# Decoder trunk on one core: block sums planned earlier in a second tile, a weight sum formed from other regions, and the first w_o weights asked for inside the branch loop

## The chip, the core and the metric

The kernel runs on one core of a Trainium2 chip. The metric is device time in microseconds (us): the median over runs of the whole kernel, one launch each. Engines are named as in the profile: PE (matrix products), PEld (weight loads of PE), DVE, ACT and POOL (elementwise work), SP (it issues the transfers; its queue reads SPq in the trace).

## The reference

Two layers of a decoder trunk run over a sequence of 1024 with a model width of 1024. Each layer has a mixer and a gated feed-forward part.

```python
def rmsnorm(x, g):
    y = xf * lax.rsqrt(jnp.mean(xf * xf, axis=-1, keepdims=True) + RMS_EPS)
    return (y * g).astype(x.dtype)
...
D_MODEL = 1024; SEQ = 1024; DEPTH = 2; HEAD_DIM = 64; D_FF = 2816
DSW_GROUPS = ((128, 1), (512, 4), (2048, 16))     # (window, dilation), 4 heads each
SB_HEADS = 4                                      # stick-breaking heads
...
# mixer, per layer:
#   h = rmsnorm(x, norm1) ; one projection w_in gives q/k/v of both branches and two gates
#   branch A: softmax attention in dilated windows with ALiBi, three groups mixed by their denominators
#   branch B: A[t,s] = sigmoid(z_ts) * prod_{s<j<t} (1 - sigmoid(z_tj)), o = A v
#   m = sigmoid(gate_a) * (o_a @ w_br[:OUT_A]) + sigmoid(gate_b) * (o_b @ w_br[OUT_A:])
#   x = x + m @ w_o
# feed-forward: up-projection, depthwise conv of the gate half, GELU, down-projection
```

All of it is in 32-bit floating point.

## The kernel before

**Precision.** Each fp32 operand is split into two parts of the type fp32r, `hi = copy(x)` on ACT (L129) and `lo = x - hi` on DVE (L130), by the helper `split`; a product of two operands is three matmuls (`hi*hi`, `lo*hi`, `hi*lo`). `piece(src)` splits a 128x512 region of weights into two new tiles.

**Tiles.** `H[n]` holds the normalised input h of token half n as `hh`, `hl`. Tiles come from pools by tag, and a new tile of a tag waits until the oldest buffer of that tag is no longer used. The tag "xa" has four buffers of 128x2048 (here: `h_sum`, and `on`, `ob_in`), "wr" two (`NRAW`; raw weights `w_raw`, `br_raw`, and the tile `u` of the pairs), "ql" two (`in_a`), "ot" is a tag with a single 128x1024 buffer (here: the zeros `none`, and `raw_c` at the start of a layer).

**The mixer.** Attention is cut into items: B00 to B17 (stick-breaking), N00 to N11 (near windows), T00 to T17 (far windows). `attend` goes through them and, between their steps, advances a `Dense` object, which yields the projections one matmul group at a time. PE's order is written out by hand in this way; the rows of PE are kept in the order of the program, while the other engines' instructions outside the feed-forward part are placed by a list scheduler. At each advance `aside()` takes one entry off the list `side`, if the item that the entry names is done.

**The pairs.** 28 pairs of projections (keys and queries, values, gates) go by a seven-product scheme on 2x2 blocks. One of the seven products is computed early by `ahead` and kept in DRAM. `pair_rest` computes the other six from the four 128x512 regions a11, a12, a21, a22 of the tile `in_a`: it forms weight sums on POOL and DVE, splits them (w6, w5, w7, then w3, w4), and multiplies them by sums of h. A pair's third weight sum, for w7, is made by POOL on L998, in the half `u2` of the tile `u`; the other half `u1` receives the kept product from DRAM. L1000 is `a21 += a22` (POOL), L1003 `a11 = a21 - a11` (DVE), L1006 `a11 = a12 - a11` (POOL). L855 is four copies (`fx`) that a far item puts on POOL.

**The sums of h.** `block_sums` fills `dense.side`: for each of the sums S[3], S[1], S[2], S[4] four items of 128x512. An item of S[3] and S[1] is three POOL operations (L906 to L908, function `first`) into one quarter of the tile `h_sum`, an item of S[2] and S[4] two DVE operations on that tile (L917, L918, `further`). `in_two` then splits the quarter into the tiles t_hi and t_lo. In `series(after, t, f, lag, gap)` item i starts at entry i*gap and is split at entry i*gap+lag, once the item named by `after` is done.

**The branches.** After the far items come the products with `w_br` (`br_raw`, four loads by `branch_in`, L1214), the gates read back from DRAM (`gin`, L1206) and, in layer 0, `residual_in`. The loop goes over 16 outputs i. Then come the products with `w_o`, whose weights are loaded in pieces by L140 in `wo_chunk`; the first step of the generator `wo[0]` asks for the first two of them and splits them.

Of the kernel before, what the change touches and what calls it, by code (L numbers as in the profile page):

```python
# [6 lines left out]
F32 = mybir.dt.float32  # L7
# [4 lines left out]
ALU = mybir.AluOpType  # L12
# [3 lines left out]
P = 128  # L16
T = 1024
D = 1024
KD = D // P
HF = 512  # L20
# [11 lines left out]
NRAW = 2  # L32
# [20 lines left out]
def trunk_kernel(ctx, tc, x, norm1, w_in, b_gate, w_br, w_o, norm2, w_up, conv_w, conv_b, w_down, norm_f, out, depth=None, probe=None):  # L53
    nc = tc.nc
    act, dve, pe, pool = nc.scalar, nc.vector, nc.tensor, nc.gpsimd
# [4 lines left out]
    sb = ctx.enter_context(tc.tile_pool(name="sb", bufs=1))  # L60
# [64 lines left out]
    def quarter(name, dtype=F32, c=HF):  # L125
        return sb.tile([P, 2048 // c, c], dtype, tag="xa", bufs=4, name=name)

    def split(hi, lo, src):
        act.copy(hi, src)  # L129
        dve.tensor_tensor(lo, src, f32(hi), ALU.subtract)  # L130
# [64 lines left out]
    class Dense:  # L195
# [29 lines left out]
        def at(self, ahead, f):  # L225
            self.later.setdefault(self.count + ahead, []).append(f)
# [203 lines left out]
    S, B = {}, {}  # L430
# [15 lines left out]
    def new_s(t):  # L446
        hi, lo = big("t_hi", F32R), big("t_lo", F32R)
        S[t] = [tuple(x.rearrange("p a (b c) -> p (a b) c", c=HF)[:, i, :] for x in (hi, lo)) for i in range(4)]
# [431 lines left out]
    def piece(src):  # L880
        hi = sb.tile([P, 512], F32R, tag="wh", bufs=4, name="w_hi")
        lo = sb.tile([P, 512], F32R, tag="wl", bufs=4, name="w_lo")
        split(hi, lo, src)
        return hi, lo
# [10 lines left out]
    def block_sums():  # L895


        keep = {}

        def first(t, a, b, i):  # L900
            if i == 0:
                if "r" not in keep:
                    keep["r"] = quarter("h_sum")
                new_s(t)
            r, (ah, al), (bh, bl) = keep["r"][:, i, :], a()[i], b()[i]
            pool.tensor_tensor(r, f32(al), f32(bl), ALU.subtract)  # L906
            pool.tensor_tensor(r, r, f32(ah), ALU.add)
            pool.tensor_tensor(r, r, f32(bh), ALU.subtract)  # L908

        def further(t, a, i):  # L910
            if t == 4:

                S[4] = half(0, 0)
            elif i == 0:
                new_s(t)
            r, (ah, al) = keep["r"][:, i, :], a()[i]
            dve.tensor_tensor(r, f32(ah), r, ALU.subtract)  # L917
            dve.tensor_tensor(r, r, f32(al), ALU.add)  # L918

        def in_two(t, i):  # L920
            split(*S[t][i], keep["r"][:, i, :])

        b11, b12, b21, b22 = (lambda n=n, k=k: half(n, k) for k in range(2) for n in (1, 0))
        todo = []

        def series(after, t, f, lag, gap):

            at = {}
            for i in range(4):
                at.setdefault(i * gap, []).append(lambda i=i: f(i))  # L930
                at.setdefault(i * gap + lag, []).append(lambda i=i: in_two(t, i))
            for k in range(3 * gap + lag + 1):
                todo.append((after, lambda fs=at.get(k, ()): [g() for g in fs]))

        series({"B17"}, 3, lambda i: first(3, b22, b12, i), 6, 5)
        series({"N01s"}, 1, lambda i: first(1, b12, b11, i), 6, 5)
        series({"N11s"}, 2, lambda i: further(2, b22, i), 1, 1)
        series({"plain", "01", "v0"}, 4, lambda i: further(4, b21, i), 1, 1)
        return todo

# [37 lines left out]
    def pair_rest(dense, l, offs, put, view, grid, kept):  # L978
        raw = []

        def load():
            raw.append(sb.tile([P, 4, 512], F32, tag="ql", bufs=2, name="in_a"))
            for c in range(2):
                nc.sync.dma_start(
                    raw[0][:, 2 * c : 2 * c + 2, :].rearrange("p a (k n) -> p (a k) n", n=P),
                    w_in[l][:, offs[c] : offs[c] + P].rearrange("(k p) n -> p k n", p=P),
                )

        def run():
            if not raw:  # L990
                assert dense.loads.pop(0) is load
                load()
            a11, a12, a21, a22 = (raw[0][:, i, :] for i in range(4))
            yield
            u = sb.tile([P, T], F32, tag="wr", bufs=NRAW, name="u")
            u1, u2 = u[:, HF:T], u[:, 0:HF]
            nc.sync.dma_start(u1, kept)
            pool.tensor_tensor(u2, a11, a21, ALU.subtract)  # L998
            yield
            pool.tensor_tensor(a21, a21, a22, ALU.add)  # L1000
            yield
            yield
            dve.tensor_tensor(a11, a21, a11, ALU.subtract)  # L1003
            w6 = piece(a11)
            yield
            pool.tensor_tensor(a11, a12, a11, ALU.subtract)  # L1006
            w5 = piece(a21)
            yield
            w7 = piece(u2)
            yield  # L1010
            u5 = small("u5")
            pa, pc = bank("ps", "i_a"), bank("ps", "i_c")
            yield from seven(pa, w6, S[2], True, True)
            r2 = u2
            dve.tensor_tensor(view(r2), view(u1), grid(pa), ALU.add)
            w3 = piece(a11)
            yield "turn"
            yield
            yield from seven(pc, w5, S[1], True, True)
            dve.tensor_tensor(view(u5), view(u1), grid(pc), ALU.add)  # L1020
            w4 = piece(a22)
            if dense.loads:
                dense.loads.pop(0)()
            dense.last(0)
            yield "turn"
            yield
            yield from seven(pa, w7, S[3], False, True)
            dve.tensor_tensor(view(u5), view(u5), grid(pa), ALU.add)
            put(1, 0, u5, False)
            yield "turn"  # L1030
            yield
            yield from seven(pc, w3, half(0, 1), False, True)
            dve.tensor_tensor(view(r2), view(r2), grid(pc), ALU.add)
            put(0, 0, r2, False)
            dense.last(1)
            yield "turn"
            yield
            for word in seven(pa, w4, S[4], False, True):
                yield "turn"
                yield  # L1040
            dve.tensor_tensor(view(u1), view(u1), grid(pa), ALU.add)
            put(1, 1, u1, False)
            yield

        return run, load
# [84 lines left out]
    def mixer(l, pending):  # L1130
# [58 lines left out]
        def in_two(nm):  # L1189
            for src in (R["ob" if nm == "b" else "on"],):  # L1190
                hi, lo = big("oh_" + nm, F32R), big("ol_" + nm, F32R)
                for n in range(2):
                    for c in range(2):
                        sl = slice(n * HF, (n + 1) * HF)
                        split(hi[:, c, sl], lo[:, c, sl], src[:, c, sl])
                oh[nm] = (hi, lo)

        branches()
        todo = [(n, e0 + i) for e0 in range(0, KD, 2) for n in range(2) for i in range(2)]
# [25 lines left out]
        wo = [wo_chunk(l, n, e) for n in range(2) for e in range(KD)]  # L1225
# [5 lines left out]
        if l == 0:  # L1231
            for n in range(2):
                new_x(n)
        next(wo[0])
        next(residual, None)

        order = [(i, ab) for ab in (1, 0) for i in range(AHEAD_B)]
# [2 lines left out]
        for i, ab in order:  # L1240
            n, e = todo[i]
            sl = slice(n * HF, (n + 1) * HF)
            if i not in seen:
                if e == 0:
                    new_h(n)
                if i % 4 == 0:
                    wb = wbs.pop(0)
                if l and i in X_AT:
                    x_in(X_AT.index(i) // 2, X_AT.index(i) % 2)
            gt = gts[i]  # L1250
            ec = slice((e % 2) * P, (e % 2 + 1) * P)
            if "ab"[ab] not in oh:
                in_two("a")
            o = bank("st"[ab], "br_ps")
            (wh, wl), (xh, xl) = wb[ab], oh["ab"[ab]]
            for _ in product(o, [((wh[:, c, ec], wl[:, c, ec]), (xh[:, c, sl], xl[:, c, sl])) for c in range(2)]):
                pass
            with tc.high_priority(offset=AHEAD):
                dve.tensor_tensor(gt[:, ab, :], gt[:, ab, :], o, ALU.mult)
            seen[i] = seen.get(i, 0) + 1  # L1260
            if seen[i] == 1:
                continue
            m = small("mrg")
            dve.tensor_tensor(m, gt[:, 0, :], gt[:, 1, :], ALU.add)
            late.append((n, e, m))
            if len(late) > 1:
                merged(*late.pop(0))
            gate_in(i + 3)
            if i % 4 == 1:
                branch_in(i + 3)  # L1270
            next(residual, None)
# [586 lines left out]
```

## Time and profile before

| | before |
|---|---|
| median of 3 runs | 2748.46 us (2747.33 to 2750.36) |
| profiled execution | 2750.43 us |
| its span | 2748.6 us |
| mean granted PE clock | 0.993 |
| PE busy | 2672.8 us, 97% |
| DVE busy | 2096.1 us, 76% |
| ACT busy | 1328.1 us, 48% |
| POOL busy | 694.2 us, 25% |

PE is busy nearly all of the span, so a change can shorten the kernel only by the time that PE waits, by PE running at a higher granted clock, or by less work for PE. The work on PE is the same in both kernels. Rows of the timeline read: start in us, duration in us, engine, line, operation, output <- input, size, count, and in brackets the idle time of that engine just before with what ended it.

### The profile page before, as it was taken

What the parts mean: (1) busy time and instruction counts of PE and PEld (TensorE: products, weight loads), DVE (VectorE), ACT (ScalarE), POOL (GpSimd) and SP (SyncE); (2) the same over time, 40 slices, a digit from 0 to 9 for tenths busy, and PEclk for the clock granted to TensorE, in tenths of its full rate; (3) what the DMA queues carried; (4) which work ended last, traced back from release to release, by engine and by line L of the source; (5) the groups of instructions that cost most, each with busy time, mean ns of one, the idle gap of its engine ahead of it and who ended that gap; (6) DMA issues with size and microseconds to landing.
All of it is one profiled execution on the core that took longest, in us unless ns stands there. A gap on an engine that the chain in (4) does not pass through costs nothing. (4 is left out here: it accounts for less than half of the span.)

```text
span 2748.6 us, 36975 instructions
## 1 busy us (share of the span) xinstructions
PE 2672.8 (97%) x13098; PEld 2232.0 (81%) x13098; DVE 2096.1 (76%) x3132; ACT 1328.1 (48%) x2458; POOL 694.2 (25%) x509
## 2 busy tenths in 40 slices
PE   8998999999999999999999989999899999999999
PEld 8877777888888888888888778878788888888888
DVE  5887866775689888897658877666758888988865
ACT  5665534455455545432345655334545455554225
POOL 1004122212224433321210051221222333443110
PEclk9999999999999999999999999999999999999999
DMA  4023379764334443688411234897632434446863
GB/s 152 26 85 108 121 215 238 197 206 148 88 123 149 150 155 139 218 325 318 157 35 47 81 100 136 238 233 196 226 103 79 143 139 164 156 143 245 332 250 123
DMA packets 397637, 445.72 MB, mean 162 GB/s; under 512 B 21660, under 2 KB 318988, under 8 KB 395916
## 3 DMA queue, kind: packets, MB, share of 16 engines
q1 hardware_dynamic: 397452, 443.35, 50.4%
q8 instruction: 104, 1.70, 0.3%
q14 instruction: 81, 0.66, 0.1%
HBM read 300.61 MB, written 142.67 MB: 161 GB/s over the span
## 5 line engine op out<-in xcount | busy, mean ns | idle before, releaser
L130 DVE TENSOR_TENSOR w_lo<-up_a,w_hi 128x512 fp32r<-128x512 f32 x240 | 236.8, 993 | 20.1 <-ACT w_hi L129 20.1
L129 ACT CAST w_hi<-up_a 128x512 fp32r<-128x512 f32 x240 | 149.4, 623 | 183.8 <-PE u_a L890 45.8
L1614 DVE TENSOR_TENSOR x<-x,d_ps 128x512 f32<-128x512 f32 (+1 forms) x228 | 152.2, 671 | 78.1 <-PE d_ps L1608 77.3
L1345 POOL TENSOR_TENSOR cv<-cv 128x512 f32<-128x512 f32 x88 | 131.8, 1508 | 248.6 <-DVE cv L1340 138.7
L130 DVE TENSOR_TENSOR w_lo<-w_raw,w_hi 128x512 fp32r<-128x512 f32 x176 | 126.0, 719 | 68.8 <-ACT w_hi L129 68.3
L129 ACT CAST w_hi<-w_raw 128x512 fp32r<-128x512 f32 x176 | 109.2, 621 | 135.4 <-PE o_ps L156 66.5
L130 DVE TENSOR_TENSOR g<-cv,g 128x512 fp32r<-128x512 f32 x154 | 152.3, 990 | 5.3 <-ACT g L129 2.8
L129 ACT CAST w_hi<-in_a 128x512 fp32r<-128x512 f32 x112 | 68.6, 619 | 130.6 <-PE i_a L890 58.2
L1606 PE MATMUL d_ps<-gd_in,w_hi 128*128 128x512 f32 (+1 forms) x340 | 130.1, 383 | 1.5 <-ACT w_hi L129 1.2
L1608 PE MATMUL d_ps<-gd_in,w_lo 128*128 128x512 f32 (+1 forms) x340 | 129.8, 382 | 0.0
L1607 PE MATMUL d_ps<-gd_in,w_hi 128*128 128x512 f32 (+1 forms) x340 | 129.8, 382 | 0.0
L889 PE MATMUL u_a<-hh,w_hi 128*128 128x512 f32 x320 | 124.6, 389 | 0.3 <-DVE u L1496 0.3
L890 PE MATMUL u_a<-hl,w_hi 128*128 128x512 f32 x320 | 124.5, 389 | 0.0
L891 PE MATMUL u_a<-hh,w_lo 128*128 128x512 f32 x320 | 124.5, 389 | 0.0
L889 PE MATMUL u_a<-t_hi,w_hi 128*128 128x512 f32 x320 | 124.5, 389 | 0.0
L890 PE MATMUL u_a<-t_lo,w_hi 128*128 128x512 f32 x320 | 124.5, 389 | 0.0
L891 PE MATMUL u_a<-t_hi,w_lo 128*128 128x512 f32 x320 | 124.5, 389 | 0.0
L998 POOL TENSOR_TENSOR u<-in_a 128x512 f32<-128x512 f32 x28 | 37.9, 1355 | 328.1 <-DMA gs<-u 102.4
L1606 PE MATMUL d_ps<-gd_in,wd 128*128 128x512 f32 (+1 forms) x292 | 113.9, 390 | 0.0
L129 ACT CAST g<-cv 128x512 fp32r<-128x512 f32 x154 | 94.9, 616 | 38.0 <-POOL cv L1345 29.6
L1608 PE MATMUL d_ps<-gd_in,wd 128*128 128x512 f32 (+1 forms) x292 | 112.8, 386 | 0.0
L1607 PE MATMUL d_ps<-gd_in,wd 128*128 128x512 f32 (+1 forms) x292 | 112.8, 386 | 0.0
(390 smaller groups left out, 8715.4 us busy)
## 6 DMA issues: line engine op xcount, KB each, us to landing
gd<-g SPq DMA_DIRECT2D x154, 512.0 KB, 3.6
gd_in<-gd SPq DMA_DIRECT2D x154, 512.0 KB, 6.4
up_a<-in_w_up_dram SPq DMA_DIRECT2D x80, 512.0 KB, 5.3
in_a<-in_w_in_dram SPq DMA_DIRECT2D x56, 512.0 KB, 5.8
w_raw<-in_w_in_dram SPq DMA_DIRECT2D x104, 256.0 KB, 3.0
t_kq<-tk SPq DMA_DIRECT2D x64, 384.0 KB, 6.9
wd_raw<-in_w_down_dram SPq DMA_DIRECT2D x22, 1024.0 KB, 13.3
gin<-gs SPq DMA_DIRECT2D x32, 512.0 KB, 4.4
```

The costliest lines, as they stand in the source:

```text
L129: act.copy(hi, src)
L130: dve.tensor_tensor(lo, src, f32(hi), ALU.subtract)
L889: pe.matmul(o, w[0][:, c], rh, start=(first and i == 0), stop=False, skip_group_check=True)
L890: pe.matmul(o, w[0][:, c], rl, start=False, stop=False, skip_group_check=True)
L891: pe.matmul(o, w[1][:, c], rh, start=False, stop=(last and i == 3), skip_group_check=True)
L998: pool.tensor_tensor(u2, a11, a21, ALU.subtract)
L1345: return lambda: pool.tensor_tensor(dst, a, b, ALU.subtract)
L1606: pe.matmul(o[:, sub], wh[:, c], gh[:, sub], start=(i == 0 and k in (0, 4, 5)), stop=False, skip_group_check=True)
L1607: pe.matmul(o[:, sub], wh[:, c], gl[:, sub], start=False, stop=False, skip_group_check=True)
L1608: pe.matmul(o[:, sub], wl[:, c], gh[:, sub], start=False, stop=(i == m - 1), skip_group_check=True)
L1614: dve.tensor_tensor(x, x, o[:, sub], ALU.add)
```

## The change

1. **Sums of h.** The items 0 and 1 of S[3] go into a new tile `h_sum2` of the tag "ot" and are planned after item B14; items 2 and 3 stay in `h_sum` after B17, and the splits of all four get an explicit plan. The sums of S[1] get a lag of 7 and a gap of 6 in place of 6 and 5. The tiles t_hi and t_lo are allocated by the first split.
2. **Pairs.** The POOL operation `u2 = a11 - a21` is gone. After w6 (`a11 = a21 + a22 - a11`) POOL does `a12 -= a11` and `a11 = a22 - a11`, which is the old a11 - a21 again, and w7 is split from a11, w3 from a12. The tile `u` and the load of its half `u1` are asked for two steps later than the first operation was.
3. **Branches.** The first step of `wo[0]` is taken at i = 11 in the loop, not ahead of the loop.

```diff
         keep = {}
+        S.clear()
+
+        def at(t, i):
+            if t == 3 and i < 2:
+                if "o" not in keep:
+                    keep["o"] = sb.tile([P, 2, HF], F32, tag="ot", name="h_sum2")
+                return keep["o"][:, i, :]
+            if "r" not in keep:
+                keep["r"] = quarter("h_sum")
+            return keep["r"][:, i, :]
 
         def first(t, a, b, i):
-            if i == 0:
-                if "r" not in keep:
-                    keep["r"] = quarter("h_sum")
-                new_s(t)
-            r, (ah, al), (bh, bl) = keep["r"][:, i, :], a()[i], b()[i]
+            r, (ah, al), (bh, bl) = at(t, i), a()[i], b()[i]
...
         def in_two(t, i):
-            split(*S[t][i], keep["r"][:, i, :])
+            if t not in S:
+                new_s(t)
+            split(*S[t][i], at(t, i))
...
-        series({"B17"}, 3, lambda i: first(3, b22, b12, i), 6, 5)
-        series({"N01s"}, 1, lambda i: first(1, b12, b11, i), 6, 5)
+        plan({"B14"}, {0: [third(0)], 6: [third(1)]})
+        plan({"B17"}, {0: [third(2)], 1: [cast(0)], 4: [cast(1)], 6: [third(3)], 9: [cast(2)], 14: [cast(3)]})
+        series({"N01s"}, 1, lambda i: first(1, b12, b11, i), 7, 6)
         series({"N11s"}, 2, lambda i: further(2, b22, i), 1, 1)
...
             a11, a12, a21, a22 = (raw[0][:, i, :] for i in range(4))
             yield
+            pool.tensor_tensor(a21, a21, a22, ALU.add)
+            yield
+            yield
+            dve.tensor_tensor(a11, a21, a11, ALU.subtract)
+            w6 = piece(a11)
+            yield
+            pool.tensor_tensor(a12, a12, a11, ALU.subtract)
+            pool.tensor_tensor(a11, a22, a11, ALU.subtract)
+            w5 = piece(a21)
+            yield
             u = sb.tile([P, T], F32, tag="wr", bufs=NRAW, name="u")
             u1, u2 = u[:, HF:T], u[:, 0:HF]
             nc.sync.dma_start(u1, kept)
-            pool.tensor_tensor(u2, a11, a21, ALU.subtract)
-            yield
-            pool.tensor_tensor(a21, a21, a22, ALU.add)
-            yield
-            yield
-            dve.tensor_tensor(a11, a21, a11, ALU.subtract)
-            w6 = piece(a11)
-            yield
-            pool.tensor_tensor(a11, a12, a11, ALU.subtract)
-            w5 = piece(a21)
-            yield
-            w7 = piece(u2)
+            yield
+            w7 = piece(a11)
             yield
...
-            w3 = piece(a11)
+            w3 = piece(a12)
...
-        next(wo[0])
         next(residual, None)
...
             late.append((n, e, m))
+            if i == 11:
+                next(wo[0])
             if len(late) > 1:
```

In the changed kernel the lines have other numbers: L906 to L908 are L912 to L914, L944 is L960, L1000 is L1011, L1006 is L1017, the new POOL operation is L1018, L1003 is L1014, L1102, L1206 and L1214 are L1118, L1222 and L1230.

The first place is POOL in layer 0, from the zeros `none` to the first sums of h. The `ql` memsets are four tiles of the items' queries; `hl_109`, `hh_108` are the parts of H[0] and `hl_363` is one of H[1]. POOL before:

```order
L944 MEMSET none 128x1024
L545 MEMSET ql 64x1024
L546 MEMSET ql 64x1024
L545 MEMSET ql 64x1024
L546 MEMSET ql 64x1024
L906 TENSOR_TENSOR h_sum<-hl_109 128x512 x2
L907 TENSOR_TENSOR h_sum<-h_sum,hh_108 128x512 x2
L908 TENSOR_TENSOR h_sum<-h_sum,hh_108 128x512 x2
L906 TENSOR_TENSOR h_sum<-hl_109 128x512 x2
L907 TENSOR_TENSOR h_sum<-h_sum,hh_108 128x512 x2
L908 TENSOR_TENSOR h_sum<-h_sum,hh_108 128x512 x2
```

The same place on POOL after the change:

```order
L960 MEMSET none 128x1024
L912 TENSOR_TENSOR h_sum_2248<-hl_109 128x512 x2
L913 TENSOR_TENSOR h_sum_2248<-h_sum_2248,hh_108 128x512 x2
L914 TENSOR_TENSOR h_sum_2248<-h_sum_2248,hh_108 128x512 x2
L545 MEMSET ql 64x1024
L546 MEMSET ql 64x1024
L545 MEMSET ql 64x1024
L546 MEMSET ql 64x1024
L912 TENSOR_TENSOR h_sum<-hl_109 128x512 x2
L913 TENSOR_TENSOR h_sum<-h_sum,hh_108 128x512 x2
L914 TENSOR_TENSOR h_sum<-h_sum,hh_108 128x512 x2
```

Six operations, those of two items of S[3], stand ahead of the four memsets now, right behind the zeros; behind the memsets are 18 sum operations in place of 24.

The second place is POOL among the pairs of layer 0, where the first far item's four `fx` copies stand. POOL before:

```order
L1000 TENSOR_TENSOR in_a<-in_a 128x512
L1006 TENSOR_TENSOR in_a<-in_a 128x512
L998 TENSOR_TENSOR u<-in_a 128x512
L1000 TENSOR_TENSOR in_a<-in_a 128x512
L1006 TENSOR_TENSOR in_a<-in_a 128x512
L855 COPY fx<-sf 128x8x64 x4
L998 TENSOR_TENSOR u<-in_a 128x512
```

The same place on POOL after the change:

```order
L1011 TENSOR_TENSOR in_a<-in_a 128x512
L1017 TENSOR_TENSOR in_a<-in_a 128x512
L1018 TENSOR_TENSOR in_a<-in_a 128x512
L1011 TENSOR_TENSOR in_a<-in_a 128x512
L1017 TENSOR_TENSOR in_a<-in_a 128x512
L855 COPY fx<-sf 128x8x64 x4
L1018 TENSOR_TENSOR in_a<-in_a 128x512
```

A pair's three operations are now L1011, L1017, L1018, all on `in_a`, and the four `fx` copies stand between the second and the third operation of a pair instead of between two pairs.

The third place is SP at the change from the pairs to the branches in layer 1: `gs` takes the gates to DRAM, `x` reads the residual back, `w_raw` is a first w_o load. SP before:

```order
L1102 DMA gs<-u 128x512
L140 DMA w_raw<-in_w_o_dram 128x4x128
L404 DMA x_18173<-xs_86 128x2048
L1102 DMA gs<-u 128x512
L140 DMA w_raw<-in_w_o_dram 128x4x128
L1214 DMA br_raw<-in_w_br_dram 128x4x256
L1206 DMA gin<-gs 128x1024 x3
L1214 DMA br_raw<-in_w_br_dram 128x4x256
L1206 DMA gin<-gs 128x1024
L1214 DMA br_raw<-in_w_br_dram 128x4x256
```

The same place on SP after the change:

```order
L1118 DMA gs<-u 128x512
L1230 DMA br_raw<-in_w_br_dram 128x4x256
L1118 DMA gs<-u 128x512
L404 DMA x_18163<-xs_86 128x2048
L1230 DMA br_raw<-in_w_br_dram 128x4x256 x2
L1222 DMA gin<-gs 128x1024 x4
L140 DMA w_raw<-in_w_o_dram 128x4x128
L1222 DMA gin<-gs 128x1024 x2
L140 DMA w_raw<-in_w_o_dram 128x4x128
```

The last three `br_raw` loads now stand ahead of the four `gin` loads, and both w_o loads behind them.

More of the change, by code (lines that the diff above doesn't have):

```diff
@@ L913, in further @@
                 S[4] = half(0, 0)
-            elif i == 0:
-                new_s(t)
             r, (ah, al) = keep["r"][:, i, :], a()[i]
@@ L920, in in_two, with plan, third, cast @@
         def in_two(t, i):
-            split(*S[t][i], keep["r"][:, i, :])
+            if t not in S:
+                new_s(t)
+            split(*S[t][i], at(t, i))
         b11, b12, b21, b22 = (lambda n=n, k=k: half(n, k) for k in range(2) for n in (1, 0))
         todo = []
+        def plan(after, steps):
+            for k in range(max(steps) + 1):
+                todo.append((after, lambda fs=steps.get(k, ()): [g() for g in fs]))
         def series(after, t, f, lag, gap):
-            at = {}
+            steps = {}
             for i in range(4):
[L930 to L933, printed above, removed]
-        series({"B17"}, 3, lambda i: first(3, b22, b12, i), 6, 5)
-        series({"N01s"}, 1, lambda i: first(1, b12, b11, i), 6, 5)
+                steps.setdefault(i * gap, []).append(lambda i=i: f(i))
+                steps.setdefault(i * gap + lag, []).append(lambda i=i: in_two(t, i))
+            plan(after, steps)
+        def third(i):
+            return lambda: first(3, b22, b12, i)
+        def cast(i):
+            return lambda: in_two(3, i)
+        plan({"B14"}, {0: [third(0)], 6: [third(1)]})
+        plan({"B17"}, {0: [third(2)], 1: [cast(0)], 4: [cast(1)], 6: [third(3)], 9: [cast(2)], 14: [cast(3)]})
+        series({"N01s"}, 1, lambda i: first(1, b12, b11, i), 7, 6)
         series({"N11s"}, 2, lambda i: further(2, b22, i), 1, 1)
@@ L994, in run @@
             yield
[L995 to L998, printed above, removed]
-            yield
             pool.tensor_tensor(a21, a21, a22, ALU.add)
@@ L1005, in run @@
             yield
-            pool.tensor_tensor(a11, a12, a11, ALU.subtract)
+            pool.tensor_tensor(a12, a12, a11, ALU.subtract)
+            pool.tensor_tensor(a11, a22, a11, ALU.subtract)
             w5 = piece(a21)
             yield
-            w7 = piece(u2)
+            u = sb.tile([P, T], F32, tag="wr", bufs=NRAW, name="u")
+            u1, u2 = u[:, HF:T], u[:, 0:HF]
+            nc.sync.dma_start(u1, kept)
+            yield
+            w7 = piece(a11)
             yield
```

## The prediction

> **What bounds the kernel now.** I read the page first, then the list of PE's waits, then the timelines of POOL, ACT and PE at the three places that the change touches.
>
> ```profile
> PE 2672.8 (97%) x13098; PEld 2232.0 (81%) x13098; DVE 2096.1 (76%) x3132; ACT 1328.1 (48%) x2458; POOL 694.2 (25%) x509
> ```
>
> PE bounds the kernel: of the span of 2748.6 us it is idle for about 76. Its own instructions stay as they are, in the same order, so the change can win only parts of those 76 us and of the time in which PE ran at a lower granted clock. The list of its waits (engine, line, what it waited for: us in total, times, longest) says which of them the change can reach.
>
> ```profile
> PE z L584 <- DVE st L797: 8.0, 11, 1.3
> PE o L713 <- ACT p0h L129: 6.4, 2, 3.2
> PE o L815 <- DVE p1l L130: 6.1, 7, 1.8
> ```
>
> L713 is in the near items; L584 and L815 are mostly in the far items beside the pairs. Each is an attention operand that came late, and the question is why ACT and DVE were late with it.
>
> **Part 1, the sums of h.** POOL's timeline in layer 0:
>
> ```profile
> 30.94 0.96 POOL L944 MEMSET none<- 128x1024 f32 x1 [1.42 <-issue]
> 242.43 2.54 POOL L906 TENSOR_TENSOR h_sum<-hl 128x512 f32<-128x512 f32 x2 [21.15 <-PE sb_o L649]
> 255.84 2.53 POOL L908 TENSOR_TENSOR h_sum<-h_sum,hh 128x512 f32<-128x512 f32 x2
> 274.15 1.30 POOL L908 TENSOR_TENSOR h_sum<-h_sum,hh 128x512 f32<-128x512 f32 x1
> ```
>
> POOL has nothing of the sums to do until 242.43, when the last stick-breaking item releases the buffer, and then does all 24 sum operations in one burst to 275.45. ACT takes its queue in order, and the splits of the sums stand among the splits of the near items' probabilities; ACT, then PE:
>
> ```profile
> 257.16 0.62 ACT L129 CAST t_hi<-h_sum 128x512 fp32r<-128x512 f32 x1 [5.78 <-POOL h_sum L908]
> 261.65 0.48 ACT L129 CAST p0h<-t 128x384 fp32r<-128x384 f32 x1
> 258.56 0.39 PE L157 MATMUL q_ps<-hh,w_lo 128*128 128x512 f32 x1
> 262.18 0.58 PE L713 MATMUL o<-p0h,v 128*128 128x256 f32 x1 [3.23 <-ACT p0h L129]
> 264.03 0.58 PE L713 MATMUL o<-p0l,v 128*128 128x256 f32 x1 [1.26 <-DVE p0l L130]
> 266.11 0.63 PE L156 MATMUL q_ps<-hl,w_hi 128*128 128x512 f32 x1
> 268.78 0.48 PE L155 MATMUL q_ps<-hh,w_hi 128*128 128x512 f32 x1
> 282.30 0.79 PE L155 MATMUL r_ps<-hh,w_hi 128*128 128x512 f32 x1 [1.10 <-ACT q1s L967]
> 285.52 0.54 PE L155 MATMUL r_ps<-hh,w_hi 128*128 128x512 f32 x1
> ```
>
> ACT stands 5.78 us for a sum at 257.16, so p0h is cast only at 261.65, and PE has nothing from 258.95 on. Behind the wait PE runs slowly:
>
> ```profile
> 260.00:270.00 10.00, 6.56 (x23) 5.38 (x24) 8.60 (x19) 5.64 (x15) 10.00 (x7) 0.66 0.63 202
> 280.00:290.00 10.00, 8.31 (x35) 6.78 (x36) 9.24 (x16) 4.34 (x8) 0.00 (x0) 0.83 0.34 108
> 1640.00:1650.00 10.00, 8.32 (x45) 6.64 (x44) 9.89 (x18) 5.79 (x12) 0.00 (x0) 1.00 0.35 106
> ```
>
> These windows list the busy times of PE, PEld, DVE, ACT and POOL, then the granted clock, the DMA share and GB/s. The granted clock is 0.66 and 0.83 in the two windows of layer 0, and a matmul takes 0.63 in place of 0.39. The loss of the first stop, from the rows: 258.56 to 262.18 is 3.62, less the 0.23 that such a matmul takes in a full stream (start to start, 0.39 being its latency), 3.39; 262.18 to 264.03 is 1.85, less about 0.12 for half the columns, 1.73; the 4.75 from 264.03 to 268.78 at 0.43 a matmul in place of 0.23 lose 4.75 x (1 - 0.23/0.43) = 2.2. Together 7.3. Layer 1 has the same stop:
>
> ```profile
> 1624.13 0.58 PE L713 MATMUL o<-p0h,v 128*128 128x256 f32 x1 [3.21 <-ACT p0h L129]
> 1625.98 0.58 PE L713 MATMUL o<-p0l,v 128*128 128x256 f32 x1 [1.27 <-DVE p0l L130]
> ```
>
> so 14.6 for both. A second stop stands about 282.30: the window 280 to 290 has 1.69 us of idle PE, and its 3.22 us of slow matmuls (to 285.52) lose 3.22 x 0.465 = 1.5 (0.465 is 1 - 0.23/0.43), so 3.2; in layer 1 the window 1640 to 1650 has 1.68 of idle PE and a clock of 1.00. Together 4.9. This stop is DVE's work (9.24 and 9.89 of 10 busy), which stays, but POOL's burst ends about 8 us earlier now and takes DVE's share of it along, so I take half: 2.4.
>
> After the change six operations (two items) are done behind the zeros, more than 100 us before, and their splits wait for nothing. The cast that stood 5.78 us belongs to an item whose sum is now the first pair in the burst, or done; so the stop goes. The burst is 18 operations of about 1.3, some 24 us, so it ends near 267. What is new: in layer 1 the early sums take the tile "ot" when the vectors' transposes have left it, at the head of the layer, beside stick-breaking work on DVE. There is a row for such company:
>
> ```profile
> L130 DVE TENSOR_TENSOR t_lo<-h_sum,t_hi x24: 676/686/1755, 249.4 to 1684.8; 128x512 fp32r<-128x512 f32 x24
> ```
>
> A subtraction of two SBUF operands takes 0.686 and up to 1.755 beside POOL. Six early operations can delay six such by up to 1.07 each, 6.4 in all, of which PE's queued work hides a part. I take 1.5, bounds 0 and 6.4. Part 1: 14.6 + 2.4 - 1.5 = 15.5, bounds 8 (one layer's stop comes back) and 14.6 + 4.9 = 19.5.
>
> The Trainium skill, "SBUF — State Buffer", Who interferes with whom, says that a GpSimd instruction reading SBUF and a DVE instruction with two SBUF inputs exclude each other for a whole instruction, and whoever issues first wins; the row's 1.755 against 0.686 is about one POOL operation more, so the trace agrees. By it alone all six would cost a full operation, 6.4 in place of 1.5, and the sum would be 4.9 later, 2724.4. The same skill, "TensorE: Matmul & The Clock Gate", Part 1, has the clock fall to half only after an idle window of about 3.4 us; the drop at 282.30 came behind 1.10 us of waiting, so the measurement decides. By the page the 1.5 us of slow matmuls would not be there to win, and the sum would be later by half of it, 0.75.
>
> **Part 2, the pairs.** POOL's wait for `u`, DVE's for POOL, ACT's for DVE (us in total, times, longest where given):
>
> ```profile
> DVE in_a L1003 <- POOL in_a L1000: 38.6, 22, 4.3
> POOL u L998 <- DMA gs<-u: 102.4, 10, 13.8
> 478.67 0.69 DVE L1003 TENSOR_TENSOR in_a<-in_a 128x512 f32<-128x512 f32 x1 [2.54 <-POOL in_a L1000]
> 479.76 0.33 PE L584 MATMUL z<-t_kq 128*128 128x128 f32 x1 [1.29 <-DVE st L797]
> ```
>
> L998 needs a free "wr" buffer and stands ahead of L1000 on POOL; L1003 waits for L1000, and DVE's queue behind L1003 for it. At 478.67 one sees the end: PE waits 1.29 for a result that stood behind L1003. In after L1011 is first and needs no buffer. PE's two waits of this kind sum to 8.0 + 6.1 = 14.1; some of the 18 do not follow such an L1003. I take 11.5, bounds 4 and 14.1.
>
> New: w7 now needs L1018, which needs L1017 and the split of w6. At 1.30 for each POOL operation and 0.62 + 0.69 for the split the sum is ready some 0.69 + 1.31 + 1.30 = 3.3 us behind the start of L1003, in the best case. In the two rows on the cast of w7 below that cast comes 1.90 and 8.98 behind L1003; I count the tight ones at nothing, since L1003 itself comes earlier by such as the 2.99 that it waited there (0 to 1.4 for each if it does not). In one pair per layer the `fx` copies come between:
>
> ```profile
> 388.19 0.69 DVE L1003 TENSOR_TENSOR in_a<-in_a 128x512 f32<-128x512 f32 x1 [2.99 <-POOL in_a L1000]
> 390.09 0.61 ACT L129 CAST w_hi<-u 128x512 fp32r<-128x512 f32 x1
> 482.48 1.30 POOL L1006 TENSOR_TENSOR in_a<-in_a 128x512 f32<-128x512 f32 x1 [3.85 <-DVE w_lo L130]
> 487.74 2.74 POOL L855 COPY fx<-sf 128x512 f32<-128x512 f32 x4 [3.96 <-DVE sf L849]
> 487.65 0.62 ACT L129 CAST w_hi<-u 128x512 fp32r<-128x512 f32 x1 [1.92 <-PE i_c L890]
> ```
>
> `fx` ends at 490.48, L1018 at about 491.8, so w7's cast is 4.2 later than 487.65 and the casts of the far item's probabilities behind it on ACT as well; queued matmuls hide a part, and I take 2 for PE, near the middle of 0 and 4.2, in each layer: -4. Part 2: 11.5 - 4 = 7.5, bounds 4 - 8.4 = -4 and 14.
>
> **Part 3, the branches.** Layer 1, ACT, SP and PE:
>
> ```profile
> 1956.82 0.62 ACT L129 CAST w_hi<-w_raw 128x512 fp32r<-128x512 f32 x1 [5.58 <-DMA w_raw<-in_w_o_dram]
> 1962.77 0.62 ACT L129 CAST w_hi<-w_raw 128x512 fp32r<-128x512 f32 x1 [5.33 <-DMA w_raw<-in_w_o_dram]
> 1966.37 1.13 ACT L129 CAST br_w<-br_raw 128x512 fp32r<-128x512 f32 x2
> 1961.91 0.38 SPq L1214 DMA_DIRECT2D br_raw<-in_w_br_dram  x1
> 1967.56 0.50 PE L155 MATMUL br_ps<-oh_a,br_w 128*128 128x512 f32 x1 [3.10 <-ACT br_w L129]
> 1970.57 0.79 PE L157 MATMUL br_ps<-oh_a,br_w 128*128 128x512 f32 x1 [2.28 <-DVE br_w L130]
> 1975.00 0.52 PE L155 MATMUL br_ps<-oh_a,br_w 128*128 128x512 f32 x1
> ```
>
> ACT waits twice over 5 us for w_o weights that nobody needs yet, `br_raw` gets its buffer only at 1961.91, and PE waits 3.10 and 2.28, then runs slowly for 4.43 us. The loss is about 3.27 + 2.45 + 4.43 x 0.465 = 7.8 (0.17 of issue in each of the two). In after `br_raw` takes the buffer that the first w_o load had, some 9 us earlier. But three of these loads stand ahead of the four `gin` on SP's queue, the last waits for the splits of an earlier one, and the gates read by `gin` could be late. I leave 1.8 for it: 6, bounds 2 and 7.8. The w_o weights are asked for at i = 11 and used only behind i = 15, past four outputs of twelve matmuls, 48 x 0.23 = 11 us, against the 5.58 that ACT waited for such weights: nothing there. In layer 0 no such wait stands, nothing.
>
> **The sum.** 15.5 + 7.5 + 6 = 29.0 off 2750.43: 2721.4 for an execution like the profiled one. That was 1.97 above the median of the runs, 2748.46, so I predict 2719.5. The bounds of the parts together give a gain of 6 to 41; all at one end is unlikely, so the forecast's own range is 2708 to 2730.
>
> **The rivals.** *Smaller gain.* The sums' wait only moves: ACT and DVE are close to full between 242 and 285 (DVE 8.60 and 9.24 of 10), part 1 gives 8; SP's queue with three `br_raw` ahead of `gin` gives the branch stop back, 2; the pairs gain 3.5. Sum 13.5: 2735. *Larger gain.* The second stop goes whole, `fx` costs nothing because PE has work queued: 19.5 + 11.5 + 7.8 = 38.8: 2709.5. *Slower.* In every pair the cast of w7 now stands in ACT's queue behind a POOL sum that needs w6's split and one more operation, and behind w7 stand the far items' casts. If POOL is late in most of 28 pairs and PE loses 2 us each, that is 56 against the 33 that the rest gains (29.0 and the 4 already counted here): 23 slower, 2771. It decides from 33 / 28 = 1.2 us a pair. For it: ACT waited 55.9 us in all on L1003's result, by this row,
>
> ```profile
>   ACT w_hi L129: 55.9, 13
> ```
>
> so ACT's queue does stand for pair weights; against it: POOL is busy for 25% of the span, and in the quoted pair the cast has 8.98 us. *No effect.* What PE gains here it waits for a few us later at the next item: 2747.
>
> **How the numbers follow.** Forecast 0.50, smaller gain 0.18, larger 0.10, slower 0.15, no effect 0.05, something else 0.02, faster or slower. A measurement of this kernel tells about 0.2%, 5.5 us, from no change. The first three are faster by more, 0.80 with some of the rest; no effect is same, 0.05; slower 0.15. The range for 8 in 10 takes in the first three cases and reaches a little below the larger one: 2706 to 2739.
>
> **What would show it.** In the trace of after: the cast t_hi near 257 waits for less than 1 us, no wait of 3 us for p0h in the near items of either layer, and clock 1.00 in 260 to 270. The L1014 of the pairs wait for POOL under 10 us in all, against 38.6. ACT waits under 4 us for POOL L1018 except at `fx`, once a layer. In the branches of layer 1 no ACT wait for w_raw, and PE's two waits under 2 us together. The forecast is wrong if casts of w7 wait for POOL in many pairs and the far items' products behind them, or if a stop of 3 us with its slow matmuls stands in the near items as before.

## The result and the profile after

| | before | after |
|---|---|---|
| median of 16 runs | 2748.47 us (2745.29 to 2753.52) | 2756.39 us (2750.31 to 2766.18) |
| profiled execution | 2750.43 us | 2750.49 us |
| span | 2748.6 us | 2748.7 us |
| mean granted PE clock | 0.993 | 0.994 |

The changed kernel is slower: ratio 1.0027, 95% interval 1.0017 to 1.0036, some 8 us. The prediction was 29 us faster. The two profiled executions are equally long, because that of after is one of its shortest (5.9 under its median) and that of before lies 2.0 above its median. So the two traces show where time moved, and the size is taken from the medians.

PE's order is the same in both kernels, so the start of every matmul can be set against the start of the same matmul in the other trace. How far after lies behind before at several places:

```
place (time in before)                    after lies behind by
 240   before the near items, layer 0         0.5
 300   behind them                           -6.7
 640   behind the pairs, layer 0             -0.3
1420   head of layer 1                       -0.3
1440   20 us later                           +3.9
1620   before the near items, layer 1        +3.8
1660   behind them                           -1.8
1960   behind the pairs, layer 1             +7.6
1980   in the branches, layer 1              -0.6
2740   end                                   +0.1
```

The near items and the branches won 7, 6 and 8 us, as meant. The head of layer 1 lost 4, and the pairs lost 6 and 9. The list of PE's waits says the same (engine, line, what for: us in total, times, longest):

```profile
PE o L815 <- DVE p1l L130: 23.8, 16, 4.4
PE z L584 <- DVE st L797: 5.0, 2, 2.8
PE o L713 <- DVE p0l L130: 3.7, 8, 0.6
PE o L713 <- ACT p0h L129: 1.2, 2, 0.6
```

The wait for p0h fell from 6.4 to 1.2, the two of br_ps for weights are gone, but the wait for p1l in the far items rose from 6.1 to 23.8. The windows of after answer to those of before (busy times of PE, PEld, DVE, ACT, POOL, then granted clock, DMA share, GB/s):

```profile
260.00:270.00 10.00, 9.41 (x50) 7.53 (x49) 7.16 (x17) 8.07 (x20) 9.55 (x8) 1.00 0.50 134
460.00:470.00 10.00, 6.81 (x22) 5.25 (x21) 4.93 (x7) 1.20 (x2) 2.56 (x2) 0.69 0.41 125
500.00:510.00 10.00, 5.60 (x28) 4.64 (x28) 4.58 (x9) 3.19 (x9) 2.68 (x3) 0.91 0.89 217
1960.00:1970.00 10.00, 9.93 (x44) 7.94 (x43) 7.01 (x12) 2.16 (x4) 0.96 (x1) 1.00 0.90 291
```

Between 260 and 270 PE is now busy for 9.41 at full clock (6.56 at 0.66 before), between 1960 and 1970 for 9.93 (5.08). The new stops stand among the pairs: 460 to 470 at a clock of 0.69, and 500 to 510. This is the first one, on POOL, DVE, ACT and PE of after:

```profile
460.06 1.29 POOL L1011 TENSOR_TENSOR in_a<-in_a 128x512 f32<-128x512 f32 x1 [7.03 <-DMA in_a<-in_w_in_dram]
461.39 0.69 DVE L1014 TENSOR_TENSOR in_a<-in_a 128x512 f32<-128x512 f32 x1 [4.49 <-POOL in_a L1011]
457.98 0.48 ACT L129 CAST p1h<-t 128x384 fp32r<-128x384 f32 x1 [0.32 <-PE t L807]
463.89 0.54 DVE L130 TENSOR_TENSOR p1l<-t,p1h 128x384 fp32r<-128x384 f32 x1
464.49 0.58 PE L815 MATMUL o<-p1l,t_v 128*128 128x256 f32 x1 [3.19 <-DVE p1l L130]
466.15 0.63 PE L891 MATMUL i_a<-t_hi,w_lo 128*128 128x512 f32 x1
```

Read from below: PE waits 3.19 for p1l and then runs at 0.63 a matmul; p1l stands on DVE behind the difference L1014, though its own input p1h is there from 458.46 on; L1014 stands 4.49 for the sum L1011; and L1011 waits for the transfer that brings the pair's weights. The waits of the difference and of the first sum in the whole run, and of the third sum:

```profile
DVE in_a L1014 <- POOL in_a L1011: 57.5, 21, 4.5
POOL in_a L1011 <- DMA in_a<-in_w_in_dram: 104.0, 24, 10.3
POOL in_a L1018 <- DVE w_lo L130: 294.4, 28, 35.8
```

Before, the sum L1000 did not wait for the transfer but came later, behind L998 and its buffer. Now it stands some 17 us earlier (460.06; the same pair's L1000 is at 477.4 before) and reaches the weights while they are under way. Why DVE stands there is seen in DVE's order, around the difference of that pair (the tenth). Before:

```
L130 TENSOR_TENSOR p1l<-t_4720,p1h 128x384
L1033 TENSOR_TENSOR u<-u,i_c 128x512
L130 TENSOR_TENSOR w_lo<-u,w_hi 128x512
L130 TENSOR_TENSOR p1l<-t_4745,p1h 128x384
L1041 TENSOR_TENSOR u<-u,i_a 128x512
L130 TENSOR_TENSOR w_lo<-in_a,w_hi 128x512
L600 TENSOR_TENSOR ot<-o_4709,fold 64x512
L1015 TENSOR_TENSOR u<-u,i_a 128x512
L130 TENSOR_TENSOR w_lo<-in_a,w_hi 128x512
L1003 TENSOR_TENSOR in_a<-in_a 128x512
```

After:

```
L130 TENSOR_TENSOR p1l<-t_4723,p1h 128x384
L1014 TENSOR_TENSOR in_a<-in_a 128x512
L1049 TENSOR_TENSOR u<-u,i_c 128x512
L130 TENSOR_TENSOR w_lo<-in_a,w_hi 128x512
L130 TENSOR_TENSOR p1l<-t_4749,p1h 128x384
```

The difference moved up past eight operations of the pair before it and of the far item, p1l among them. The list scheduler put it where its sum seemed ready; the ring of two buffers of the tag "wr", from which u comes, had held both back, as the runs below show.

The head of layer 1, on DVE and POOL of after:

```profile
1427.76 2.56 POOL L913 TENSOR_TENSOR h_sum<-h_sum,hh 128x512 f32<-128x512 f32 x2
1429.11 1.49 DVE L627 TENSOR_TENSOR_SCAN stay<-stay,zero 128x128 f32<-128x128 f32 x1 [0.22 <-ACT stay L625]
1430.63 1.20 DVE L628 TENSOR_TENSOR beta<-beta,stay 128x127 f32<-128x127 f32 x1
1431.76 1.75 DVE L627 TENSOR_TENSOR_SCAN stay<-stay,zero 128x256 f32<-128x256 f32 x1
```

And the same three operations of DVE before:

```profile
1429.44 0.42 DVE L627 TENSOR_TENSOR_SCAN stay<-stay,zero 128x128 f32<-128x128 f32 x1 [0.22 <-ACT stay L625]
1429.90 0.29 DVE L628 TENSOR_TENSOR beta<-beta,stay 128x127 f32<-128x127 f32 x1
1430.11 0.68 DVE L627 TENSOR_TENSOR_SCAN stay<-stay,zero 128x256 f32<-128x256 f32 x1
```

Beside POOL's early sums the three take 4.44 in place of 1.39.

### The profile page after: what moved, and what is told of

The parts are those of the page before. It is cut to its first block, busy times and chain, and to the rows that moved or that the text cites. A ratio compares the mean times of both kernels' runs of the same rounds, so it can differ in the third digit from the quotient of the medians.

```text
span 2748.7 us, 36983 instructions
## 1 busy us (share of the span) xinstructions
PE 2669.9 (97%) x13098; PEld 2233.4 (81%) x13098; DVE 2098.8 (76%) x3132; ACT 1330.0 (48%) x2458; POOL 699.0 (25%) x509
## 5 line engine op out<-in xcount | busy, mean ns | idle before, releaser
L130 DVE TENSOR_TENSOR w_lo<-w_raw,w_hi 128x512 fp32r<-128x512 f32 x176 | 131.5, 751 | 65.7 <-ACT w_hi L129 65.2
L129 ACT CAST w_hi<-in_a 128x512 fp32r<-128x512 f32 x140 | 86.8, 620 | 156.9 <-PE i_a L890 80.9
L1623 PE MATMUL d_ps<-gd_in,wd 128*128 128x512 f32 (+1 forms) x292 | 113.9, 390 | 0.0
L627 DVE TENSOR_TENSOR_SCAN stay<-stay,zero 128x128 f32<-128x128 f32 (+3 forms) x64 | 89.0, 1390 | 32.6 <-ACT stay L625 32.0
L1018 POOL TENSOR_TENSOR in_a<-in_a 128x512 f32<-128x512 f32 x28 | 38.3, 1369 | 294.4 <-DVE w_lo L130 294.4
L1625 PE MATMUL d_ps<-gd_in,wd 128*128 128x512 f32 (+1 forms) x292 | 112.8, 386 | 0.0
```

The lines of the kernel that those rows point to most:

```text
L627: dve.tensor_tensor_scan(rev, rev, zero[:, 0:1].to_broadcast([P, L]), 1.0, ALU.mult, ALU.add)
L1018: pool.tensor_tensor(a11, a22, a11, ALU.subtract)
L1623: pe.matmul(o[:, sub], wh[:, c], gh[:, sub], start=(i == 0 and k in (0, 4, 5)), stop=False, skip_group_check=True)
L1625: pe.matmul(o[:, sub], wl[:, c], gh[:, sub], start=False, stop=(i == m - 1), skip_group_check=True)
```

## The experiments

Each kernel was timed in five rounds beside the kernel before; medians, with the ratio to before and its 95% interval.

**One part alone.** Three kernels have one part of the diff each.

> The kernel before with the pairs' edit alone. By the matched starts of PE's matmuls in the two traces, the changed kernel loses 6.3 us between 300 and 640 (layer 0) and 10.5 between 1660 and 1960 (layer 1). If the pairs' edit makes that loss by itself, under either theory of how, this kernel is 17 us slower than before, 2765 (2757 to 2772), ratio about 1.006. If the loss comes of the sums' edit (another state of DVE and ACT when the pairs begin) or of w_o, it is within 4 us of 2748.

> The kernel before with the sums' edit alone. By the same matching the near items gain 7.1 in layer 0 and 6.1 in layer 1, and the head of layer 1 loses 4.2 to the early sums: 9 us faster than before, 2739 (2735 to 2744), ratio 0.9967. If the gain of the near items is given back in the pairs whatever their order is, it is within 3 us of 2748.

> The kernel before with the w_o edit alone: the stop at 1964 in layer 1 goes and nothing else changes, 7.5 us faster than before, 2741 (2738 to 2745), ratio 0.9973. If that stop was only slack that a later wait takes, 2748.

| part alone | median | ratio to before |
|---|---|---|
| pairs | 2775.61 | 1.0098 (1.0082 to 1.0113) |
| sums of h | 2739.28 | 0.9964 (0.9953 to 0.9976) |
| w_o weights | 2742.42 | 0.9973 (0.9965 to 0.9982) |

The pairs' edit loses 27 us by itself, more than its expected range; the other two win 9.5 and 6.3 as expected. Together that would be 11 us slower, against 8 measured. (By the table above the changed kernel loses 9.4 between 1660 and 1960, not 10.5 as the expectation has it.)

**The pair's steps one later.** In the changed kernel all of a pair up to w5 is written one step earlier than before. The tile u is asked for four steps later than before (the description of the change says two). This edit moves the steps up to w5 back:

```diff
             yield
+            yield
             pool.tensor_tensor(a21, a21, a22, ALU.add)
...
             nc.sync.dma_start(u1, kept)
-            yield
             w7 = piece(a11)
```

> The changed kernel with one yield moved: the pair's first POOL sum, its DVE difference, w6 and w5 stand one step later again, where the kernel before has them; the regions, the third sum on POOL behind w6 and the late tile u stay as changed. Theory one (the steps stand one step early, DVE waits in order behind the in_a load, p1l is late): the pairs' loss of 17 goes and some of the 102 us that POOL stood for u may come back as gain, 2732 (2722 to 2740). Theory two (the rival of the prediction: the third sum waits for w6's split and w7's cast holds up ACT): the loss stays, 2756 (2750 to 2763).

2759.52, ratio 1.0036 (1.0023 to 1.0049): the loss stays. But this did not decide for the rival, since the scheduler put the difference of the tenth pair at the same place on DVE all the same, between the same operations, and DVE stood as in the changed kernel (L1012 is the first sum here, L1015 the difference):

```profile
DVE in_a L1015 <- POOL in_a L1012: 57.4, 20, 5.2
```

Where an operation is written had no say here; that the scheduler goes by when its inputs seem ready is the reading that the next runs test. So the next edits give or take a reason to wait.

**The ring given back, and taken from the old kernel.** The first edit is on the changed kernel, the second on the kernel before.

```diff
             yield
+            u = sb.tile([P, T], F32, tag="wr", bufs=NRAW, name="u")
+            u1, u2 = u[:, HF:T], u[:, 0:HF]
+            nc.sync.dma_start(u1, kept)
+            yield
-            pool.tensor_tensor(a21, a21, a22, ALU.add)
+            pool.tensor_tensor(u2, a21, a22, ALU.add)
             yield
             yield
-            dve.tensor_tensor(a11, a21, a11, ALU.subtract)
+            dve.tensor_tensor(a11, u2, a11, ALU.subtract)
...
-            w5 = piece(a21)
+            w5 = piece(u2)
...
-            u = sb.tile([P, T], F32, tag="wr", bufs=NRAW, name="u")
-            u1, u2 = u[:, HF:T], u[:, 0:HF]
-            nc.sync.dma_start(u1, kept)
-            yield
             w7 = piece(a11)
```

> The changed kernel, with the first POOL sum of a pair written to u2 (the half of the tile u) in place of a21, and u asked for before it, as in the kernel before. So that sum waits for the ring of two again, and the DVE difference stands again behind the far item's L797 on DVE (it stood ahead of it in the changed kernel and in the run with the yield moved). The third sum stays on POOL behind w6's split. New theory (the ring of two had held the difference back; without it DVE reaches it while in_a is still under way, stands, and p1l with it): the pairs' loss of 24 (2756.4 less the 2732.8 that the sums' and w_o's edits alone give together) goes, 2733 (2727 to 2740). Rival (the third sum's place behind w6's split): 2756 (2750 to 2761).

```diff
-            pool.tensor_tensor(u2, a11, a21, ALU.subtract)
             yield
             pool.tensor_tensor(a21, a21, a22, ALU.add)
...
             w6 = piece(a11)
             yield
+            pool.tensor_tensor(u2, a22, a11, ALU.subtract)
             pool.tensor_tensor(a11, a12, a11, ALU.subtract)
```

> The mirror of it: the kernel before with only the order of two POOL operations turned: L1000 comes first and needs no u, the third sum goes to u2 as a22 less the difference, and stands behind it. The third sum does not overwrite a11 and so does not wait for w6's split, but L1000 and L1003 are free of the ring. New theory: the loss of the pairs' edit alone, 2775 less up to some us, 2765 to 2778. Rival (third sum behind w6's split): no loss, 2748 (2742 to 2752).

With the ring given back 2722.54, ratio 0.9904 (0.9891 to 0.9917): 34 us faster than the changed kernel. With the ring taken from the old kernel 2772.74, ratio 1.0087 (1.0074 to 1.0100): 24 us slower than before, with the third sum in a place of its own. The waits of the first (L1015 is the first sum, L1018 the difference):

```profile
POOL u L1015 <- DMA in_a<-in_w_in_dram: 0.2, 1, 0.2
DVE in_a L1018 <- POOL u L1015: 38.0, 23, 3.5
PE o L815 <- DVE p1l L130: 3.4, 6, 1.1
```

And of the second (L999 is the first sum, L1002 the difference):

```profile
POOL in_a L999 <- DMA in_a<-in_w_in_dram: 109.7, 23, 9.6
DVE in_a L1002 <- POOL in_a L999: 66.4, 20, 6.8
PE o L815 <- DVE p1l L130: 23.7, 12, 5.6
```

The wait for the transfer is 0.2 with the ring and 110 without, and PE's wait for p1l goes with it: 3.4 and 23.7. DVE's order changes with it too: with the ring the difference of the tenth pair stands behind all eight operations again, and in the old kernel without it ahead of them.

**The difference on POOL.** The changed kernel, with one engine exchanged:

```diff
-            dve.tensor_tensor(a11, a21, a11, ALU.subtract)
+            pool.tensor_tensor(a11, a21, a11, ALU.subtract)
             w6 = piece(a11)
```

> The changed kernel with the difference a11 = a21 - a11 (L1014) on POOL in place of DVE, 28 times; PE's order is the same. DVE no longer stands for POOL. New theory: p1l's waits on PE, 23.8 in the changed kernel, fall under 8 and with them the slow clock behind them: 2735 (2722 to 2745); ACT may stand instead for w6 behind POOL, which would leave part of the loss. Rival (third sum late): four POOL operations in a row make it later still, 2756 to 2765.

2718.04, ratio 0.9889 (0.9876 to 0.9902). POOL stands for the transfer as long as in the changed kernel, and next to nobody waits for it there:

```profile
POOL in_a L1011 <- DMA in_a<-in_w_in_dram: 116.4, 24, 9.6
POOL in_a L1018 <- DVE w_lo L130: 272.9, 28, 44.3
ACT w_hi L129 <- POOL in_a L1011: 2.5, 1, 2.5
PE o L815 <- DVE p1l L130: 1.1, 2, 0.9
```

This and the pair of runs above show the cause: DVE standing in its queue for a late transfer. By itself this run would not, since it also takes 28 operations of 0.69 us off DVE; the pair above moves none. The third sum still waits 272.9 for w6's split here, and the kernel is the faster for all that, so the rival is out.

**The sums and w_o without the pairs; both cures.** The first kernel is before with the other two parts, the second has the ring given back and the difference on POOL.

> The kernel before with the sums' and the w_o edit and without the pairs' edit. If the two are independent: 2748.4 - 9.5 - 6.3 = 2732.6 (2729 to 2737). It is the base for the held pairs: with it at 2733 the held pairs of 2722.5 gain about 10 over the old pairs, which would bear out the gain that the prediction set for the pairs, 11.5 less 4. If it lies near 2723, the held pairs gain nothing and the edit of the regions is worth nothing.

> Both cures at once: the first sum waits for the ring of two as before, and the difference is on POOL as well. If the two cures take away the same wait (DVE standing behind in_a), they do not add: 2717 to 2723. If the hold and the engine each take away a wait of their own, it is below both, 2712. If POOL now holds up w6 on ACT through the ring, it is above 2723.

2729.85, ratio 0.9936 (0.9924 to 0.9949), and 2714.61, ratio 0.9880 (0.9866 to 0.9893). Over the first, the held pairs of 2722.54 win 7.3, so the new regions are worth something where the ring stays. By the medians the two cures add in part: 3.4 below the better one and 7.9 below the other. The 3.4 is no more than likely, since the intervals of the two ratios overlap. With both, PE waits 1.7 for p1l, but ACT now waits 30.8 for the difference (12 times). The last is the fastest kernel of this study, 34 us under before.

**The early sums of layer 1.** Two kernels try to move them out of the first scans' way. The first is the one without the pairs' edit, where they wait for a column of B14's result; the second the one with the difference on POOL, where `raw_c` of layer 1 has a tile of the tag "p4".

```diff
...
+                if l and i < 2:
+                    act.copy(at(3, i)[64:128, 0:1], R["ob"][64:128, 1, 0:1])
                 first(3, b22, b12, i)
...
```

> The kernel before with the sums' and the w_o edit, without the pairs' edit, and in layer 1 with the two early sums held back by a copy of one column from the result of B14, so that they run where the plan names them and not at 1425 beside the first scans. Without the hold the sum of the two edits is 2748.7 - 9.5 - 6.3 = 2732.9. If the 4 us at the head of layer 1 come from POOL's sums beside DVE's scans, and the scans at B14 have more room: 2729 (2726 to 2732). If the scans there are hit as much: 2733; if the head's loss has another cause: 2733 as well, with the L627 of 1.5 us still at 1429.

> The run with the difference on POOL, and layer 1's raw vectors raw_c in a tile of the tag p4 in place of ot, so that h_sum2 is free there from the start and the early sums of layer 1 stand on POOL among the splits of the first norm, before the scans. If the head's loss of 4 is POOL's sums beside the scans L627 and L628, it goes: 2714 (2711 to 2717). If the sums now delay the norm's hl on POOL instead, and PE with it, or the loss has another cause: 2718 to 2722.

2735.51, ratio 0.9951 (0.9938 to 0.9965), and 2721.24, ratio 0.9903 (0.9888 to 0.9918): 5.7 and 3.2 slower by the medians than without these edits, with intervals that overlap. In the first the loss at the head goes (by the matched starts 3.9 against the trace without the edit) and 4.4 come back at 1570, beside a scan of more columns (POOL, DVE, PE):

```profile
1567.52 2.75 POOL L912 TENSOR_TENSOR h_sum<-hl 128x512 f32<-128x512 f32 x1
1566.59 2.58 DVE L627 TENSOR_TENSOR_SCAN stay<-stay,zero 128x768 f32<-128x768 f32 x1 [0.19 <-ACT stay L625]
1572.81 0.55 PE L638 MATMUL sb_t<-ident,beta 128*128 128x128 f32 x3 [3.42 <-DVE beta L628]
```

In the second the sums run on POOL inside the norm and hold up its last operations; PE waits, and runs at half the clock behind it:

```profile
1374.56 1.87 PE L465 MATMUL nrm_t<-ones,nrm 128*128 128x1 f32 x8 [6.45 <-POOL nrm L418]
1370.00:1380.00 10.00, 5.44 (x25) 5.44 (x26) 3.91 (x6) 3.95 (x7) 3.84 (x4) 0.51 0.50 184
```

By the matched starts this kernel lies 8.9 behind the trace without its edit at 1385 and 4.8 at 1440, so here too the head's loss of 4 goes, and more is lost ahead of it. So the loss at the head is POOL's sums beside DVE's scans, and neither place was better. The first kernel's 5.7 is not all placed: some 3 lie late in the pairs and the branches of layer 1, which were not followed up, and the profiled executions differ by 2.4 only.

## Why the prediction was wrong

**Part 1, 15.5 predicted, 9.5 measured.** The mechanism of the first stop is as described: the cast that stood 5.78 us waits no more, the clock is 1.00 between 260 and 270, and by the matched starts this stop gave 7.1 (255 to 275) and 6.1 (1620 to 1640) of the 14.6. Two terms were mis-sized. The second stop was to give 2.4 and gave nothing: PE still waits for q1s, now 1.03 where it waited 1.10, and two new small waits (0.58 and 0.43) stand ahead of it, so that after lies as far ahead at 300 as at 275.

```profile
276.65 0.50 PE L155 MATMUL r_ps<-hh,w_hi 128*128 128x512 f32 x1 [1.03 <-ACT q1s L983]
270.00:280.00 10.00, 7.90 (x38) 6.14 (x39) 9.92 (x18) 7.11 (x14) 0.69 (x1) 1.00 0.27 83
```

The other is the company of POOL at the head of layer 1: 1.5 taken, about 4 measured, inside the bounds of 0 and 6.4. The row t_lo (0.686 to 1.755, 1.07 more) had the size: the three operations shown took 0.91 to 1.07 longer each, 3.05 together. What failed is the assumption that PE's queued work hides a part, since PE lost 4.2. The 6.4 that the prediction worked out for the Trainium skill's rule ("SBUF — State Buffer", Who interferes with whom) lies a little nearer than the value taken.

**Part 2, 7.5 faster predicted, 27 slower measured** (26.9 alone; 2756.39 less 2729.85 is 26.5 beside the other two parts). The step that failed is "L1011 is first and needs no buffer". The prediction looked at the wait that ended last, the buffer, and took it for the only one. Without it the sum reached the next wait, in_a, 104.0 us in all; DVE's wait for POOL was to fall under 10 and rose from 38.6 to 57.5. The prediction showed POOL's order and not DVE's, where the difference had moved up past p1l. With the ring given back the pairs do win 7.3, but that this is near the 7.5 is luck. DVE's wait for the first sum, which was to go, is 38.0 there and 40.5 without the pairs' edit, and the 4 taken off for `fx` were not lost. PE's two waits L584 and L815 fall only from 7.5 + 5.1 to 6.2 + 3.4; where the rest of the 7.3 comes from was not followed up.

**Part 3, 6 predicted, 6.3 measured.** At the turn to the branches of layer 1 there is no wait for w_raw any more, and none of PE for br_w. The three `br_raw` ahead of `gin` cost ACT one wait of 6.34 and PE nothing:

```profile
1964.38 1.15 ACT L129 CAST br_w<-br_raw 128x512 fp32r<-128x512 f32 x2 [6.34 <-DMA br_raw<-in_w_br_dram]
```

**The rivals.** "Slower" named the right place and the right sign, but took 2 us a pair where the pairs' edit alone lost about 1 (26.9 over 28), and it had the wrong wait: of the third sum's 294.4 us of waiting nothing comes through, for ACT never waits for L1018 in the trace of after. PE's stop of 4.40 at 508 comes behind a DVE that stands 4.11 for L1011. The 4 us that the prediction expected at `fx` are not there: the copies end at 486.68, and L1018 behind them starts only at 498.85, when w6's split is done.

**The clock.** Of the pairs' loss a good part is slow running: behind the stop of 3.19 us the matmuls take 0.63 in place of 0.39 for 6 us. The Trainium skill, "TensorE: Matmul & The Clock Gate", Part 1, has the clock fall after an idle window of about 3.4 us that runs freely. The trace agrees for the stop of 4.40: PE is idle in all of the 3.41 us ahead of the slow stretch. It does not agree for the stop of 3.19, nor for the one of 1.10 before, where PE was busy for 0.88 and 1.74 of those 3.41 us and the granted clock fell to 0.50 all the same (the 3.41 us ahead of each slow stretch and the first 3.41 us of it; the first two pairs from after, the third from before):

```profile
504.80:508.21 3.41, 0.00 (x0) 0.00 (x0) 2.90 (x4) 0.00 (x0) 1.74 (x2) 1.00 0.62 155
508.21:511.62 3.41, 3.21 (x9) 2.68 (x10) 0.61 (x2) 0.00 (x0) 0.00 (x0) 0.50 0.94 202
460.42:463.83 3.41, 0.88 (x5) 0.47 (x3) 2.44 (x3) 0.62 (x1) 2.20 (x2) 1.00 0.15 54
463.83:467.24 3.41, 2.75 (x8) 2.36 (x9) 2.49 (x5) 0.58 (x1) 0.00 (x0) 0.50 0.63 159
278.84:282.25 3.41, 1.74 (x9) 1.10 (x7) 3.41 (x7) 3.31 (x6) 0.00 (x0) 1.00 0.37 109
282.25:285.66 3.41, 3.36 (x10) 2.67 (x10) 3.37 (x6) 0.00 (x0) 0.00 (x0) 0.50 0.25 91
```

So a window that is partly idle was enough here; how busy one must be was not measured. If a stop of a given length sometimes sets it off and sometimes not, that would fit the wider spread of after's runs (16 us against 8); this was not tried.

## What to carry to other kernels

A wait for a buffer can be what keeps an operation from standing at the head of an in-order queue for something later still. Before taking such a wait away, look up the next input that the operation needs and when it lands, and see on every engine that follows what the operation will then stand ahead of. If a scheduler places it by modelled readiness, give it a real dependency or an engine whose queue nobody needs; writing it a step later did nothing here.

## What was not expected of the hardware

Three operations of DVE that took 0.42, 0.29 and 0.68 us before took 1.49, 1.20 and 1.75 beside POOL operations of about 1.3 each. They lost 1.07, 0.91 and 1.07, nearly the same whatever their own length, so the short ones lost most in proportion. And a stop on PE cost more than its length where the clock fell behind it: in the layer 0 pairs, by the matched starts, the wait of 3.19 set PE back by 6.3 us against before, and that of 4.40 by 6.1.
